# Memory tokens that arrive channels first, packed weight blocks for their projection, x scaled on GpSimd with the norm weight applied at eviction, and half of x transposed between the output products

## The chip, the cores and the metric

The kernel runs on one core of one Trainium2 chip. The metric is the device time of the whole program in microseconds, the median of several executions; lower is better. The engines are named as in the profile: PE (TensorE matmul), PEld (its weight loads), DVE (VectorE), ACT (ScalarE), POOL (GpSimd) and SP (SyncE, which here issues every transfer).

## What is computed

One layer of a hybrid encoder: 1024 tokens of 1024 channels go through a mixer with four head groups (A, B, C, D) and then through cross-attention into 256 memory tokens. The change touches what comes first: the norm of `x`, the keys and values of the memory, and (in the kernel) the product of the values with the output weights.

```python
def rms_norm(x, g):
    y = x32 * lax.rsqrt(jnp.mean(x32 * x32, axis=-1, keepdims=True) + NORM_EPS)
    return (y * g).astype(x.dtype)
...
def memory_cross_attention(h, mem_n, wq, wkv, wo):
    q = split_heads(h @ wq, N_MEM_HEADS)
    k, v = jnp.split(mem_n @ wkv, 2, axis=-1)
    ...
    p = jax.nn.softmax(logits, axis=-1)
    o = jnp.einsum("bhtm,bhmd->bhtd", p.astype(v.dtype), v)
    return merge_heads(o) @ wo
```

The mixer reads `rms_norm(x, pre_norm_g)` through one projection `w_in`. `mem_n` is the memory, 256 x 1024, normed with `mem_norm_g`; `wkv` is 1024 x 2048.

## The kernel before

Every large product is made of three (`mm3`, L136 to L139): both operands are split into a rounded high part and the low rest, and high x high (L137), high x low (L138) and low x high (L139) are added up in PSUM. So each piece of a weight, 256 KB, goes a fixed way (`wload`, L111 to L127): SP loads it to a raw buffer `wr`, ACT casts it to `wh` (L122), and DVE (L124) or POOL (L126) subtracts to make `wl`; in the first stage the two take turns. There are four raw buffers and eight each of `wh` and `wl` there. `split_evac` (L158 to L164) does the same for what comes out of PSUM: ACT makes the high part, DVE the low one, with a factor per partition (L163, L164) or without (L160, L161).

The order of instructions on each engine is set by a list scheduler that follows the written order and priorities, and every engine, SP's transfers included, works strictly in that order. The part up to the mixer runs so:

1. The constants `cols` and two 512 KB row tiles of `mem` are loaded (L188 to L194). PE turns the memory round to channels first, 16 transposes (L215), and `split_evac` writes `mTh` and `mTl` with the norm weight `mg` as factor. ACT squares the row tiles (L220) for the norm of each memory token; two more transposes (L226) bring the 256 factors along the free dimension (`RS`).
2. Eight blocks `cp` (loop at L258) of 256 columns of `wkv`: four weight pieces, 48 products of 256 columns, one multiplication by `RS` (L268), then a store of keys to `kTd` (L270, blocks 0 to 3) or a split of values (blocks 4 to 7). A weight piece is cut out of rows of 2048 columns, 1 KB at a time.
3. In the same loop a tile of 128 tokens of `x` is loaded and normed (`xnorm`, L240): ACT squares and sums, POOL takes the power -0.5 (L143, L144), DVE multiplies by that and by the norm weight in one instruction (`norm_rows`, L151). One block later `xtile` (L247) transposes it, eight transposes into two PSUM banks, and `split_evac` writes `hTh` and `hTl`.
4. Four heads of `vwrow` (L325): 24 products of 512 columns each, values times `wo`, copied out by ACT (L335) and stored.
5. Then comes the first projection of the mixer, group C, which reads all of `hTh` and `hTl`.

PSUM has four banks for products (`mm`) and four for transposes (`tr`) in this stage.

Of the kernel before, what the change touches and what calls it, by code (L numbers as in the profile page):

```python
# [11 lines left out]
ALU = mybir.AluOpType  # L12
# [24 lines left out]
def tile_trunk(ctx: ExitStack, tc: tile.TileContext, a, out, dbg=None):  # L37
# [60 lines left out]
    # ---------------------------------------------------------------- helpers  # L98
# [12 lines left out]
    def wload(src, scale=None):  # L111
        shape = [src.shape[0], src.shape[1], src.shape[2]] if len(src.shape) == 3 else [src.shape[0], src.shape[1]]
        with tc.high_priority():
# [9 lines left out]
            if cur["wp0"] is not None and wcount["wr"] % 2:  # L123
                V.tensor_tensor(lo, raw, f32(hi), op=ALU.subtract)  # L124
            else:
                G.tensor_tensor(lo, raw, f32(hi), op=ALU.subtract)  # L126
# [54 lines left out]
    xp = Pool("xp", {"x": 2, "xn": 3, "gbc": 1})  # L181
    cur["wp0"] = Pool("wp0", {"wr": 2, "wh": 4, "wl": 4})

    # ---------------------------------------------------------------- first loads
    pr0 = tc.cur_priority
    tc.cur_priority = -1000
    cst = base.one("cst", [128, 206])
    SY.dma_start(cst, a["cols"])  # L188
    ident, mg = cst[:, 0:128], cst[:, 198:206]
    mx_ = []  # L190
    for i in range(2):
        x_t = xp("x", [128, 1024])
        SY.dma_start(x_t, a["mem"][0, i * 128:(i + 1) * 128, :])
        mx_.append(x_t)  # L194
# [7 lines left out]
    V.memset(mhalf, -0.5)  # L202

    # ---------------------------------------------------------------- memory side and pre norm
    mss = m0.one("mss", [128, 2])
    mTh = [m0("mT", [128, 4, 256], F32R) for _ in range(2)]
    mTl = [m0("mT", [128, 4, 256], F32R) for _ in range(2)]
    for kp in range(4):
        if kp == 1:
            tc.cur_priority = pr0  # L210
        p = ps("tr", [128, 2, 256])
        for i in range(2):
            for kk in range(2):
                k = 2 * kp + kk
                T.transpose(p[:, kk, i * 128:(i + 1) * 128], mx_[i][:, k * 128:(k + 1) * 128], ident)  # L215
        for kk in range(2):
            q, r = divmod(2 * kp + kk, 4)
            split_evac(mTh[q][:, r, :], mTl[q][:, r, :], p[:, kk, :], mg[:, 2 * kp + kk:2 * kp + kk + 1])
    for i in range(2):
        SC.activation(xp("xn", [128, 1024]), mx_[i], AF.Square, accum_out=mss[:, i:i + 1])  # L220
    mr = rstd_pow("tn", mss, D, EPS, 2)
    rE = m0.one("rE", [128, 2, 128])
    V.tensor_copy(rE, mr[:, :, None].to_broadcast([128, 2, 128]))
    p = ps("tr", [128, 256])
    for i in range(2):
        T.transpose(p[:, i * 128:(i + 1) * 128], rE[:, i, :], ident)  # L226
    RS = m0.one("RS", [128, 2, 256])
    SC.activation(RS[:, 0, :], p, AF.Copy, scale=1.0 / 16)
    SC.copy(RS[:, 1, :], p)
# [1328 lines left out]
```

## Time and profile before

| | |
|---|---|
| time, median of 3 runs | 983.16 us (980.48 to 984.74) |
| span of the profiled execution | 981.5 us (first to last instruction; no separate device time is given for it) |
| mean granted TensorE clock | 0.976 |
| PE busy in 0 to 70 us, by tens | 3.65, 8.70, 9.85, 9.27, 10.00, 10.00, 7.35 us |
| bytes moved by DMA in 0 to 90 us | 21.75 MB, 242 GB/s on average |

The profile is read from the whole to the part: the busy time of each engine over the span, then over stretches of it, then single instructions in order of time. A row of the timeline gives its start, how long it took, the engine, the line, what it wrote from what, and in brackets how long the engine sat idle before it and what ended that. Matmuls overlap, so the distance of their starts tells more than their lengths.

### The profile page before, as it was taken

Reading aid. Unit: us, or ns where it says so; the run is one execution under the profiler, and the core shown is the slowest. Engines: PE = TensorE matmul, PEld = TensorE weight load, DVE = VectorE, ACT = ScalarE, POOL = GpSimd, SP = SyncE. Lnnn points to the kernel's source line nnn. Section 1 sums busy time; section 2 is a strip of 40 time slices with the busy share of each in tenths; the row PEclk is TensorE's granted clock in tenths of the full one; section 3 lists DMA queues with packets and bytes.
Section 4 is the critical chain, followed back from the end, with each engine's and each line's share of the span. In section 5 each row is a group of like instructions: output and inputs, shape, how many; then the busy total and the mean of one; then the engine's idle time right before and its main releaser. Section 6 shows DMA issues by size and latency. Waiting matters only on the chain. (4 is left out here: it accounts for less than half of the span.)

```text
span 981.5 us, 16277 instructions
## 1 busy us (share of the span) xinstructions
PE 929.1 (95%) x6089; PEld 772.7 (79%) x6089; DVE 578.9 (59%) x1291; ACT 419.6 (43%) x974; POOL 252.9 (26%) x254
## 2 busy tenths in 40 slices
PE   6989999797998999999898999999999999999997
PEld 6987887586778877777776776777778788889997
DVE  6773136788696135794498747655556546654226
ACT  6666255231154333653435245433345434443321
POOL 4554224452220224454233412000000000121211
PEclk9999999798999999999899999999999999999999
DMA  7867321102324402322566675432217311125104
GB/s 241 265 212 262 107 54 34 32 22 72 75 66 123 115 28 87 111 80 87 150 158 159 198 258 188 131 100 76 75 46 245 105 35 55 44 67 198 38 12 172
DMA packets 94447, 112.53 MB, mean 115 GB/s; under 512 B 20705, under 2 KB 72993, under 8 KB 94369
## 3 DMA queue, kind: packets, MB, share of 16 engines
q1 hardware_dynamic: 94368, 111.50, 36.5%
q8 instruction: 48, 0.79, 0.3%
q14 instruction: 31, 0.25, 0.1%
HBM read 82.61 MB, written 28.87 MB: 114 GB/s over the span
## 5 line engine op out<-in xcount | busy, mean ns | idle before, releaser
L126 POOL TENSOR_TENSOR wl<-wr,wh 128x512 fp32r<-128x512 f32 (+2 forms) x98 | 139.9, 1430 | 401.8 <-ACT wh L122 385.0
L137 PE MATMUL mm<-h,wh 128*128 128x512 f32 x528 | 219.6, 416 | 0.2 <-DVE zu L754 0.2
L139 PE MATMUL mm<-h,wl 128*128 128x512 f32 x528 | 208.8, 395 | 0.0
L138 PE MATMUL mm<-l,wh 128*128 128x512 f32 x528 | 208.6, 395 | 0.0
L137 PEld LDWEIGHTS mm<-h,wh 128*128 128x128 f32 x528 | 99.9, 189 | 24.3 <-issue 1.9
L139 PEld LDWEIGHTS mm<-h,wl 128*128 128x128 f32 x528 | 99.9, 189 | 22.9
L122 ACT CAST wh<-wr 128x512 fp32r<-128x512 f32 (+2 forms) x122 | 74.7, 619 | 97.5 <-PE mm L138 32.9
L138 PEld LDWEIGHTS mm<-l,wh 128*128 128x128 f32 x528 | 100.2, 190 | 17.4 <-issue 0.5
L137 PE MATMUL mm<-wh,act 128*128 128x256 f32 x256 | 71.7, 280 | 0.0
L138 PE MATMUL mm<-wl,act 128*128 128x256 f32 x256 | 70.9, 277 | 0.0
L139 PE MATMUL mm<-wh,act 128*128 128x256 f32 x256 | 70.8, 277 | 0.0
L137 PE MATMUL mm<-h,act 128*128 128x512 f32 x128 | 54.7, 427 | 0.0
L139 PE MATMUL mm<-h,act 128*128 128x512 f32 x128 | 50.5, 394 | 0.0
L138 PE MATMUL mm<-l,act 128*128 128x512 f32 x128 | 50.4, 394 | 0.0
L137 PEld LDWEIGHTS mm<-wh,act 128*128 128x128 f32 x256 | 48.2, 188 | 0.1
L138 PEld LDWEIGHTS mm<-wl,act 128*128 128x128 f32 x256 | 48.1, 188 | 0.0
L139 PEld LDWEIGHTS mm<-wh,act 128*128 128x128 f32 x256 | 48.0, 188 | 0.0
L137 PE MATMUL mm<-wh,h 128*128 128x260 f32 (+1 forms) x128 | 39.2, 306 | 1.5 <-DVE zu L819 1.5
L137 PE MATMUL mm<-mT,wh 128*128 128x256 f32 x128 | 37.6, 293 | 1.4 <-ACT wh L122 1.4
L139 PE MATMUL mm<-mT,wl 128*128 128x256 f32 x128 | 37.1, 290 | 1.4 <-DVE wl L124 1.4
L139 PE MATMUL mm<-wh,l 128*128 128x260 f32 (+1 forms) x128 | 38.1, 298 | 0.0
L138 PE MATMUL mm<-wl,h 128*128 128x260 f32 (+1 forms) x128 | 38.0, 297 | 0.0
(407 smaller groups left out, 2020.2 us busy)
## 6 DMA issues: line engine op xcount, KB each, us to landing
wr<-in_w_in_dram SPq DMA_DIRECT2D x50, 256.0 KB, 2.9
wr<-in_xattn_wkv_dram SPq DMA_DIRECT2D x32, 256.0 KB, 3.8
x<-in_x_dram SPq DMA_DIRECT2D x16, 512.0 KB, 4.7
x<-x1d SPq DMA_DIRECT2D x15, 512.0 KB, 5.6
wr<-in_xattn_wo_dram SPq DMA_DIRECT2D x16, 256.0 KB, 3.0
vwd<-row SPq DMA_DIRECT2D x8, 512.0 KB, 3.9
rT<-zu SPq DMA_DIRECT2D x16, 256.0 KB, 2.4
zT<-zu SPq DMA_DIRECT2D x16, 256.0 KB, 3.2
```

Of the source, the lines that this page charges most:

```text
L122: SC.copy(hi, raw)
L126: G.tensor_tensor(lo, raw, f32(hi), op=ALU.subtract)
L137: T.matmul(o, lh, rh, start=st, stop=False, skip_group_check=skip)
L138: T.matmul(o, lh, rl, start=False, stop=False, skip_group_check=skip)
L139: T.matmul(o, ll, rh, start=False, stop=sp, skip_group_check=skip)
```

## The change

The host now hands over the memory transposed (`memT`, 128 x 8 x 256) and the memory weights in blocks that lie together (`wkv`, 128 x 8 x 8 x 256, so a piece is 2 KB per partition), and `pre_norm_g` as columns beside `mem_norm_g`. The kernel splits `memT` straight from SBUF. The norm of the memory is made after the first block: ACT squares in place, DVE adds the eight channel groups up, one product with a matrix of ones sums over partitions, and ACT takes logarithm and exponential. `x` is multiplied by its row factor alone, by POOL, into one of six `xn` buffers (two of them held `memT`); the norm weight `pg` becomes the factor of `split_evac`. Transposes of `x` go by channel group, four token tiles to a bank: tokens 0 to 511 behind blocks 4 and 5, tokens 512 to 1023 behind the first two heads of `vwrow`. POOL gets one weight split in three instead of one in two in this stage. Comments and docstrings were taken out.

```diff
                 return hi, lo
             SC.copy(hi, raw)
-            if cur["wp0"] is not None and wcount["wr"] % 2:
+            if cur["wp0"] is not None and wcount["wr"] % 3:
                 V.tensor_tensor(lo, raw, f32(hi), op=ALU.subtract)
             else:
...
     psum(mm=4, tr=4)
     m0 = Pool("m0", {"mT": 4, "KV": 4, "row": 2, "kv": 2})
-    xp = Pool("xp", {"x": 2, "xn": 3, "gbc": 1})
+    xp = Pool("xp", {"x": 2, "xn": 6})
     cur["wp0"] = Pool("wp0", {"wr": 2, "wh": 4, "wl": 4})
     pr0 = tc.cur_priority
     tc.cur_priority = -1000
-    cst = base.one("cst", [128, 206])
+    tc.keep_in_program_order(SC.preload_act_table_set("natural_log_exp_and_others"))
+    cst = base.one("cst", [128, 214])
     SY.dma_start(cst, a["cols"])
-    ident, mg = cst[:, 0:128], cst[:, 198:206]
-    mx_ = []
-    for i in range(2):
-        x_t = xp("x", [128, 1024])
-        SY.dma_start(x_t, a["mem"][0, i * 128:(i + 1) * 128, :])
-        mx_.append(x_t)
+    ident, mg, pg = cst[:, 0:128], cst[:, 198:206], cst[:, 206:214]
+    mraw = [xp("xn", [128, 4, 256]) for _ in range(2)]
+    wv = a["wkv"]
+    wk0 = []
+    for q in range(4):
+        SY.dma_start(mraw[q // 2][:, q % 2 * 2:q % 2 * 2 + 2, :], a["memT"][:, 2 * q:2 * q + 2, :])
+        wk0.append(wload(wv[:, 0, 2 * q:2 * q + 2, :]))
     jp = m0.one("jp", [128, 128], mybir.dt.int32)
     G.iota(jp, pattern=[[1, 128]], base=0, channel_multiplier=-1)
...
     mhalf = base.one("mhalf", [128, 4])
     V.memset(mhalf, -0.5)
-    mss = m0.one("mss", [128, 2])
+    onesa = m0.one("onesa", [128, 128])
+    V.memset(onesa, 1.0)
     mTh = [m0("mT", [128, 4, 256], F32R) for _ in range(2)]
     mTl = [m0("mT", [128, 4, 256], F32R) for _ in range(2)]
-    for kp in range(4):
-        if kp == 1:
-            tc.cur_priority = pr0
-        p = ps("tr", [128, 2, 256])
-        for i in range(2):
-            for kk in range(2):
-                k = 2 * kp + kk
-                T.transpose(p[:, kk, i * 128:(i + 1) * 128], mx_[i][:, k * 128:(k + 1) * 128], ident)
-        for kk in range(2):
-            q, r = divmod(2 * kp + kk, 4)
-            split_evac(mTh[q][:, r, :], mTl[q][:, r, :], p[:, kk, :], mg[:, 2 * kp + kk:2 * kp + kk + 1])
-    for i in range(2):
-        SC.activation(xp("xn", [128, 1024]), mx_[i], AF.Square, accum_out=mss[:, i:i + 1])
-    mr = rstd_pow("tn", mss, D, EPS, 2)
-    rE = m0.one("rE", [128, 2, 128])
-    V.tensor_copy(rE, mr[:, :, None].to_broadcast([128, 2, 128]))
-    p = ps("tr", [128, 256])
-    for i in range(2):
-        T.transpose(p[:, i * 128:(i + 1) * 128], rE[:, i, :], ident)
+    for k in range(8):
+        q, r = divmod(k, 4)
+        split_evac(mTh[q][:, r, :], mTl[q][:, r, :], mraw[q][:, r, :], mg[:, k:k + 1])
+    tc.cur_priority = pr0
     RS = m0.one("RS", [128, 2, 256])
-    SC.activation(RS[:, 0, :], p, AF.Copy, scale=1.0 / 16)
-    SC.copy(RS[:, 1, :], p)
-    pg = gload(xp, "gbc", a["pre_norm_g"][0])
+    def memnorm():
+        for q in range(2):
+            SC.activation(mraw[q], mraw[q], AF.Square)
+        V.tensor_tensor(mraw[0], mraw[0], mraw[1], op=ALU.add)
+        V.tensor_tensor(mraw[0][:, 0:2], mraw[0][:, 0:2], mraw[0][:, 2:4], op=ALU.add)
+        V.tensor_tensor(mraw[0][:, 0], mraw[0][:, 0], mraw[0][:, 1], op=ALU.add)
+        p = ps("tr", [128, 256])
+        T.matmul(p, onesa, mraw[0][:, 0], start=True, stop=True)
+        SC.activation(RS[:, 1, :], p, AF.Ln, bias=eps_n, scale=1.0 / D)
+        SC.activation(RS[:, 1, :], RS[:, 1, :], AF.Exp, scale=-0.5)
+        SC.activation(RS[:, 0, :], RS[:, 1, :], AF.Copy, scale=1.0 / 16)
     hTh = [hT("h", [128, 4, 512], F32R) for _ in range(4)]
     hTl = [hT("l", [128, 4, 512], F32R) for _ in range(4)]
...
         SY.dma_start(x_t, a["x"][0, i * 128:(i + 1) * 128, :])
         xn = xp("xn", [128, 1024])
-        norm_rows(x_t, pg, xn)
-        return xn
-    def xtile(i, xn):
-        ts = slice(i % 4 * 128, (i % 4 + 1) * 128)
-        for q in range(2):
+        r = base("tn", [128, 1])
+        SC.activation(xn, x_t, AF.Square, accum_out=r)
+        r = rstd_pow("tn", r, D, EPS)
+        G.tensor_scalar(xn, x_t, r, None, op0=ALU.mult)
+        xn_.append(xn)
+    def xhalf(hf, k0, nk):
+        for k in range(k0, k0 + nk):
             p = ps("tr", [128, 4, 128])
-            for k in range(4):
-                T.transpose(p[:, k, :], xn[:, (4 * q + k) * 128:(4 * q + k + 1) * 128], ident)
-            w = 2 * (i // 4) + q
-            split_evac(hTh[w][:, :, ts], hTl[w][:, :, ts], p)
+            for i in range(4):
+                T.transpose(p[:, i, :], xn_[4 * hf + i][:, k * 128:(k + 1) * 128], ident)
+            w = 2 * hf + k // 4
+            split_evac(hTh[w][:, k % 4, :], hTl[w][:, k % 4, :], p.rearrange("p a b -> p (a b)"), pg[:, k:k + 1])
     Vh = [m0("KV", [128, 4, 256], F32R) for _ in range(2)]
     Vl = [m0("KV", [128, 4, 256], F32R) for _ in range(2)]
-    xn_ = {}
-    xn_[0] = xnorm(0)
+    xn_ = []
     for cp in range(8):
         p = ps("mm", [128, 2, 256])
-        for k, wh, wl in wpiece(a["xattn_wkv"][0], cp * 256, 256, 2):
+        for k in range(8):
+            if k % 2 == 0:
+                wp = wk0[k // 2] if cp == 0 else wload(wv[:, cp, k:k + 2, :])
+            wh, wl = (w_[:, k % 2, :] for w_ in wp)
             for c in range(2):
                 cs = slice(c * 128, (c + 1) * 128)
                 mm3(p[:, c, :], wh[:, cs], wl[:, cs], mTh[k // 4][:, k % 4, :], mTl[k // 4][:, k % 4, :],
                     k == 0 and c == 0, k == 7, True)
+        if cp == 0:
+            memnorm()
         t = m0("kv", [128, 2, 256])
         V.tensor_tensor(t, p, RS[:, cp // 4, None, :].to_broadcast([128, 2, 256]), op=ALU.mult)
...
             q, r = divmod(2 * cp - 8, 4)
             split_evac(Vh[q][:, r:r + 2, :], Vl[q][:, r:r + 2, :], t)
-        if cp < 7:
-            xn_[cp + 1] = xnorm(cp + 1)
-        if cp > 0:
-            xtile(cp - 1, xn_[cp - 1])
-    xtile(7, xn_[7])
+        xnorm(cp)
+        if cp in (4, 5):
+            xhalf(0, 4 * cp - 16, 4)
     incl = m0.one("incl", [128, 128])
     V.tensor_scalar(incl, jp, 0.0, None, op0=ALU.is_ge)
...
         nxt = vwprep(h + 1) if h < 3 else None
         vwrow(h, w)
+        if h < 2:
+            xhalf(1, 4 * h, 4)
         w = nxt
     w_in = a["w_in"][0]
...
     wp3.close()
     base.close()
-_INS = ["x", "mem", "pre_norm_g", "post_norm_g", "w_in", "b_in", "norm_a_g", "decay_w2", "iclr_a2", "gn_c_g", "gn_c_b",
-        "w_out", "xattn_post_g", "xattn_wq", "xattn_wkv", "xattn_wo", "cols", "poolbd"]
+_INS = ["x", "memT", "post_norm_g", "w_in", "b_in", "norm_a_g", "decay_w2", "iclr_a2", "gn_c_g", "gn_c_b",
+        "w_out", "xattn_post_g", "xattn_wq", "wkv", "xattn_wo", "cols", "poolbd"]
 def _pack(a):
     import numpy as np
...
             a["decay_w0"][0], a["iclr_a0"][0], a["key_k"][0], a["key_a"][0], a["bonus_u"][0],
             np.tile(a["qk_norm_d"][0], (1, 2)), b[O_AZ:O_AZ + 256], b[O_BZ:O_BZ + 256], b[O_CZ:O_CZ + 256], b[O_DZ:O_DZ + 256],
-            a["xattn_pre_g"][0], a["pool_scale"][0], b[O_DQ:O_DQ + 512], a["mem_norm_g"]]
+            a["xattn_pre_g"][0], a["pool_scale"][0], b[O_DQ:O_DQ + 512], a["mem_norm_g"], a["pre_norm_g"][0]]
     cols = np.concatenate([np.asarray(r).reshape(-1, 128) for r in rows], axis=0).T
     w = np.asarray(a["pool_w"][0])
...
         r0 = (g % 2) * 64
         pw[r0:r0 + 64, g // 2, r0:r0 + 64] = w[g]
-    return {"cols": np.concatenate([np.eye(128, dtype=cols.dtype), cols], axis=1), "poolbd": pw}
+    mt = np.asarray(a["mem"][0]).T.reshape(8, 128, 256).transpose(1, 0, 2)
+    wkv = np.asarray(a["xattn_wkv"][0]).reshape(8, 128, 8, 256).transpose(1, 2, 0, 3)
+    return {"cols": np.concatenate([np.eye(128, dtype=cols.dtype), cols], axis=1), "poolbd": pw, "memT": mt, "wkv": wkv}
 def kernel(**inputs):
```

Three places show how the order of instructions moves. In the rows, `tr`, `mm` and `KV` are banks of transposes, banks of products and the split values; the number behind a name tells buffers apart.

On ACT at the start of the program, before:

```order
L220 ACT_TABLE_LOAD
L220 ACTIVATE xn_149,mss<-x_98 128x1024
L163 ACTIVATE mT_109<-tr_113,cst 128x256
L163 ACTIVATE mT_109<-tr_122,cst 128x256
L220 ACTIVATE xn_151,mss<-x_100 128x1024
L163 ACTIVATE mT_109<-tr_113,cst 128x256
L122 CAST wh_190<-wr_188 128x512
L122 CAST wh_208<-wr_206 128x512
```

and of the change (`xn_99` and `xn_100` hold the transposed memory):

```order
L187 ACT_TABLE_LOAD
L163 ACTIVATE mT_137<-xn_99,cst 128x256 x4
L163 ACTIVATE mT_138<-xn_100,cst 128x256 x4
L122 CAST wh_104<-wr_102 128x512
L220 ACTIVATE xn_99<-xn_99 128x1024
L220 ACTIVATE xn_100<-xn_100 128x1024
L122 CAST wh_111<-wr_109 128x512
L122 CAST wh_118<-wr_116 128x512
```

All eight evictions of the memory now stand ahead of the first weight cast, where three stood, and the two Squares stand between the first cast and the second.

On PE behind the last block of the memory projection, before (`xn_748` and `xn_848` are the normed token tiles 6 and 7):

```order
L139 MATMUL mm_869<-mT_110,wl_927 128x256
L252 MATMUL tr_946<-cst,xn_748 128x128 x4
L252 MATMUL tr_953<-cst,xn_748 128x128 x4
L252 MATMUL tr_960<-cst,xn_848 128x128 x4
L252 MATMUL tr_967<-cst,xn_848 128x128 x4
L137 MATMUL mm_1057<-wh_1010,KV_174 128x512
```

and of the change, behind the first head's output products, the first of four such banks (`xn_575` to `xn_889` are token tiles 4 to 7):

```order
L139 MATMUL mm_1005<-wh_950,KV_168 128x512
L253 MATMUL tr_1014<-cst,xn_575 128x128
L253 MATMUL tr_1014<-cst,xn_689 128x128
L253 MATMUL tr_1014<-cst,xn_803 128x128
L253 MATMUL tr_1014<-cst,xn_889 128x128
L253 MATMUL tr_1021<-cst,xn_575 128x128
```

The transposes have moved from the place between the memory projection and the output products to places between heads of the output products, and each bank now takes a piece of four token tiles.

On POOL near the start, before:

```order
L126 TENSOR_TENSOR wl_209<-wr_206,wh_208 128x512
L126 TENSOR_TENSOR wl_245<-wr_242,wh_244 128x512
L143 TENSOR_SCALAR tn_183<-tn_181 128x1
L144 TENSOR_TENSOR tn_183<-tn_183,mhalf 128x1
L126 TENSOR_TENSOR wl_294<-wr_291,wh_293 128x512
```

and of the change (`x_232` and `x_317` are the raw token tiles 0 and 1):

```order
L126 TENSOR_TENSOR wl_119<-wr_116,wh_118 128x512
L143 TENSOR_SCALAR tn_237<-tn_235 128x1
L144 TENSOR_TENSOR tn_237<-tn_237,mhalf 128x1
L245 TENSOR_SCALAR xn_234<-x_232,tn_237 128x1024
L143 TENSOR_SCALAR tn_322<-tn_320 128x1
L144 TENSOR_TENSOR tn_322<-tn_322,mhalf 128x1
L245 TENSOR_SCALAR xn_319<-x_317,tn_322 128x1024
L126 TENSOR_TENSOR wl_263<-wr_260,wh_262 128x512
```

The multiply of each token tile stands behind its norm on POOL, and two of them stand ahead of the second weight split there.

## The prediction

> **What bounds the kernel now.** I read the summary of engines first, then the busy time by stretches for the first 90 us, where all edited lines run, and then the timeline of the places where TensorE (PE) is not full.
>
> ```profile
> PE 929.1 (95%) x6089; PEld 772.7 (79%) x6089; DVE 578.9 (59%) x1291; ACT 419.6 (43%) x974; POOL 252.9 (26%) x254
> ...
> 0.00:10.00 10.00, 3.65 (x16) 3.27 (x16) 3.46 (x24) 4.96 (x9) 1.00 (x8) 1.00 0.81 269
> 10.00:20.00 10.00, 8.70 (x51) 8.14 (x52) 8.04 (x12) 7.55 (x17) 5.66 (x7) 1.00 0.67 233
> ...
> 60.00:70.00 10.00, 7.35 (x63) 7.11 (x61) 8.70 (x11) 5.92 (x11) 5.97 (x5) 1.00 0.46 147
> 70.00:80.00 10.00, 8.65 (x29) 6.92 (x30) 7.99 (x12) 7.95 (x15) 3.15 (x2) 0.66 0.51 175
> ```
>
> The kernel is bound by PE, 95% busy. So I count PE time alone, up to one mark: the first product of the C projection. Behind the mark the order of instructions is row for row the same, and I take the shift of the mark as the shift of the end. In the stretches (columns behind the length: PE, weight loads, DVE, ACT, POOL, clock, DMA share, GB/s) PE is weak at two places: the first 12 us, and 60 to 80 us, where the granted clock also falls to 0.66.
>
> ```profile
> 5.28 3.65 PE L215 MATMUL tr<-cst,x 128*128 128x128 f32 x16 [5.28 <-DMA x<-in_mem_dram]
> 10.33 0.58 PE L137 MATMUL mm<-mT,wh 128*128 128x256 f32 x1 [1.40 <-ACT wh L122]
> 12.75 0.58 PE L139 MATMUL mm<-mT,wl 128*128 128x256 f32 x1 [0.52 <-DVE wl L124]
> 13.13 0.41 PE L137 MATMUL mm<-mT,wh 128*128 128x256 f32 x1
> ...
> 15.69 0.42 PE L137 MATMUL mm<-mT,wh 128*128 128x256 f32 x1
> 16.54 0.28 PE L138 MATMUL mm<-mT,wh 128*128 128x256 f32 x1
> ...
> 18.08 0.28 PE L139 MATMUL mm<-mT,wl 128*128 128x256 f32 x1
> ...
> 20.21 0.28 PE L139 MATMUL mm<-mT,wl 128*128 128x256 f32 x1
> ...
> 30.73 0.39 PE L139 MATMUL mm<-mT,wl 128*128 128x256 f32 x1 [0.88 <-DVE wl L124]
> ...
> 40.09 1.03 PE L252 MATMUL tr<-cst,xn 128*128 128x128 f32 x8
> 46.55 1.04 PE L252 MATMUL tr<-cst,xn 128*128 128x128 f32 x8
> ...
> 64.72 1.28 DVE L151 SCALAR_TENSOR_TENSOR xn<-x,tn,gbc 128x1024 f32<-128x1024 f32 x1 [0.95 <-POOL tn L144]
> 65.92 3.45 DVE L124 TENSOR_TENSOR wl<-wr,wh 128x512 fp32r<-128x512 f32 x2
> 69.30 0.68 DVE L268 TENSOR_TENSOR kv<-mm,RS 128x512 f32<-128x512 f32 x1
> 69.90 0.67 DVE L161 TENSOR_TENSOR l<-tr,h 128x512 fp32r<-128x512 f32 x1
> 70.63 0.66 PE L252 MATMUL tr<-cst,xn 128*128 128x128 f32 x4 [3.28 <-DVE l L161]
> 72.01 1.11 PE L252 MATMUL tr<-cst,xn 128*128 128x128 f32 x4 [0.72 <-DVE l L161]
> 72.77 0.78 PE L137 MATMUL mm<-wh,KV 128*128 128x512 f32 x1
> ...
> 74.20 0.63 PE L137 MATMUL mm<-wh,KV 128*128 128x512 f32 x1
> 75.48 0.63 PE L137 MATMUL mm<-wh,KV 128*128 128x512 f32 x1
> 78.01 0.40 PE L137 MATMUL mm<-wh,KV 128*128 128x512 f32 x1
> ...
> 80.11 0.40 PE L137 MATMUL mm<-wh,KV 128*128 128x512 f32 x1
> 87.12 0.40 PE L137 MATMUL mm<-wh,KV 128*128 128x512 f32 x1
> 97.62 0.39 PE L137 MATMUL mm<-h,wh 128*128 128x512 f32 x1
> ```
>
> What the reader is to see, from top to bottom:
> - The mark stands at 97.62. The first weight product of the memory projection runs at 10.33, and PE runs without a break only from 12.75, two products in.
> - Until about 16.4 a 256-wide product takes (15.69 - 13.13) / 12 = 0.213 us from start to start, afterwards (20.21 - 18.08) / 18 = 0.118: the array runs at half speed for 3.6 us of steady work. (The clock column shows 1.00 there, the starts don't.)
> - One block of 48 products and 8 transposes takes 46.55 - 40.09 = 6.46 us; 48 x 0.118 = 5.68, so a transpose is 0.10.
> - At 67.35 PE stops for 3.28 and then 0.72 us. The transposes of the last token tiles want a PSUM bank whose eviction (`l`, L161) is queued on VectorE (DVE) behind a norm multiply that waited for GpSimd, and two weight splits of 1.7 us each. After the stop the clock is halved: 512-wide products at (75.48 - 74.20) / 3 = 0.427 us until 78.0, then (87.12 - 80.11) / 30 = 0.234.
>
> PE's need at full speed is therefore 8 x 6.46 + 96 x 0.234 = 51.7 + 22.4 = 74.1 us. From 12.75 to the mark pass 84.9. Of the 10.8 in excess, the slow start holds 17 x 0.095 = 1.6, the wait at 30.73 0.9, the stop 4.0, and the slow clock behind it 12 x 0.193 = 2.3 plus about 1.0 in the transposes; 1.0 I can't place.
>
> **The change, part by part.**
>
> ```profile
> 5.17 1.06 ACT L220 ACTIVATE xn<-x 128x1024 f32<-128x1024 f32 x1 [3.17 <-DMA x<-in_mem_dram]
> ...
> L122 ACT CAST wh<-wr 128x512 fp32r<-128x512 f32 x52 | 31.4, 620 | 15.1 <-DMA wr<-in_xattn_wkv_dram 10.0 <-DMA wr<-in_w_in_dram 2.2 <-DMA wr<-in_xattn_wo_dram 1.4
> ...
> L163 ACT ACTIVATE mT<-tr,cst 128x256 fp32r<-128x256 f32 x8 | 3.4, 472 | 2.9 <-DVE mT L164 1.7 <-PE tr L215 1.2
> ...
> L124 DVE TENSOR_TENSOR wl<-wr,wh 128x512 fp32r<-128x512 f32 x24 | 27.6, 1154 | 9.1 <-ACT wh L122 9.1
> L151 DVE SCALAR_TENSOR_TENSOR xn<-x,tn,gbc 128x1024 f32<-128x1024 f32 x8 | 12.3, 1538 | 7.5 <-POOL tn L144 7.4
> ...
> L126 POOL TENSOR_TENSOR wl<-wr,wh 128x512 fp32r<-128x512 f32 x90 | 127.7, 1422 | 378.5 <-ACT wh L122 362.0 <-ACT gates L741 7.4 <-DVE wl L124 6.6
> ...
> L144 POOL TENSOR_TENSOR tn<-tn,mhalf 128x1 f32<-128x1 f32 x8 | 4.3, 541 | 0.7
> ...
> L592 POOL MEMSET n<- 128x1024 f32 x1 | 1.0, 952 | 0.0
> ```
>
> *Start.* The 16 memory transposes go (3.65 us at half speed, all before the first product). The same megabyte of `mem` lands in quarters; the row at 5.17 shows its first tile there, and I estimate the last quarter between 5.2 and 6.7 us. ACT then does eight evictions straight from SBUF, 8 x 0.47 = 3.8, from about 3.5 to 7.3 (to 7.6 if the last quarter is late), and the first cast, 0.62: the first product can start near 8.0 instead of 10.33. But ACT's next two instructions are the Squares of the memory, 1.06 each, ahead of the second cast; that cast ends near 10.7. DVE's sum of squares (1024 wide, twice the unhindered 0.68 of a 512-wide one, 1.4) holds the second low part to about 12.0. PE does the 12 products of the first piece and one or two of the second, waits about 1 us, and is continuous from 12.0 with 13 products done, against 12.75 with 2. With the same 3.6 us of slow clock that is 0.75 + 11 x 0.118 = 2.0 us ahead. Bounds: 0.5 (late quarter, a cast behind it) to 4 (clock released during the first piece).
>
> *Norm of the memory.* One ones product replaces two transposes; only the first sum waits for it, with three free PSUM banks ahead of PE. Its price on PE lies between a 256-wide start-to-start, 0.12, and the whole length of one, 0.58 at 10.33; I take 0.4, near the upper end, since its operands aren't split.
>
> *Transposes of x.* 64 before, 64 after: no PE time saved. Half stand behind blocks 4 and 5, half between the output products.
>
> *The stop at 67.35.* The norm multiply leaves DVE: 8 x 1.54 = 12.3 us. DVE takes 32 of the 48 weight splits instead of 24: 8 x 0.68 to 1.15, 5.4 to 9.2 back. What counts is the order: the last 32 transposes now follow 24 output products (5.6 us) each, and the 16 evictions of the earlier ones have blocks of 5.7 us to finish in, at about 0.6 (ACT) and 0.7 (DVE) each, four at a time. I take the whole stop, 4.0, and the slow clock behind it, 3.3, as gone. What is late next is the last scaled x tile. Tiles 6 and 7 take the buffers of tiles 0 and 1, free behind the second run of 16 transposes, by the count below at 61.0 - 2 x 5.7 = 49.6 us; two Squares, norms and multiplies of about 3.3 together follow, so they are ready near 57, and needed 5.6 us behind block 7, at 66.6.
>
> *GpSimd (POOL).* It gains eight 1024-wide multiplies by a column. No row shows one. The nearest are a 1024-wide fill at 0.95, which only writes, and the two-input split, 1.42 for 512, so 2.84 for 1024. I take 1.3, nearer the fill, since only one tensor is read. It gives up a third of its splits: 16 of 48 instead of 24. A block of 5.7 us then holds 1.33 x 1.42 + 0.8 (the norm's power at 0.54 and a smaller step ahead of it) + 1.3 = 4.0 us, at 2.84 still 5.5. Behind each multiply wait the next split on POOL and, through the raw buffer, SP's next load; behind SP's waiting load wait the x tile and the K row. I count nothing on PE, because the cover is the loader's lead: the weight pieces are two blocks deep. If that lead is gone, each late split is a PE wait of up to 2.8.
>
> [...]
>
> *Packed weights.*
>
> ```profile
> wr<-in_xattn_wkv_dram SPq DMA_DIRECT2D x32, 256.0 KB, 3.8
> wr<-in_xattn_wo_dram SPq DMA_DIRECT2D x16, 256.0 KB, 3.0
> ...
> SPq L115 <- POOL wl L126: 24.7, 15, 3.6
> ```
>
> A piece comes in 2 KB rows, as `w_out` pieces do: 3.0 us to landing instead of 3.8. SP's wait for those splits shows that the loop of four raw buffers (load, cast, split, load) is nearly as long as a block, so 0.8 less helps it keep up with blocks that shrink from 6.46 to 5.7 us. On PE: 0 to 0.9 (the wait at 30.73). I take 0.
>
> *Sum.* Start 2.0, minus 0.4, stop 4.0, clock 3.3: 8.9; a full count with no wait left (12.0 + 74.1 - 13 x 0.118 + 1.6 + 0.4 = 86.6 against 97.62; block 7 ends there at 86.6 - 22.4 - 3.2 = 61.0) gives 11.0. I forecast 9.4: of the 1.9 between them (the wait at 30.73 and the part that I can't place) most stays. The profiled span is 981.5, which lies 1.7 below the median of the runs, 983.16; no other time is given for that execution, so I take the shift off the median: **973.8 us**, about 1% less.
>
> **Rivals.**
> - *The loader falls behind* in blocks 1 to 3, which have no transposes to cover it. If the loop stays at 6.3 us, PE waits 0.6 in each, and the first split behind two x multiplies costs 2.8 more: gain 5 to 6, near 977.5. ACT's casts waiting 10 us for DMA speak for it, the two-block lead and shorter landings against.
> - *The stop comes back elsewhere.* If one of the four runs of 16 transposes (1.6 us each) must wait for a bank or the last x tile for some 3 us, the stop and the slow clock return: gain 9.4 - 7.3 = 2.1, near 981. The row at 70.63 speaks for it, the spacing above against. [...]
> - *POOL becomes the bound* (slower). Six multiplies, six norm pairs and nine splits stand ahead of the last memory split: 12.8 + 6 x 0.8 + 9 x 1.42 + 6 X = 30.3 + 6 X, needed near 59. With X the time of a multiply, the 11 us of gain are eaten at X = 6.7, and at 7.5 the kernel is near 988. That is 2.6 times the dearest row, so unlikely.
> - *More than forecast*: the clock is released early and no wait is left, gain 11 to 13, near 971.
>
> **How the numbers follow.** Forecast 0.62, loader 0.15, stop elsewhere 0.13, POOL bound 0.04, more 0.06. Half a per cent, about what a measurement of this kernel can tell from no change, is 4.9 us. Faster by more: 0.62 + 0.15 + 0.06 = 0.83; within: 0.13; slower: 0.04. The range takes in the start's bounds, the loader case and most of the upper one: 969.5 to 980.0.
>
> **What would show it.** The mark near 87 to 89 us; PE's first product near 8 with one wait of about 1 us; no PE wait of over 1 us between 13 and 85 and full-speed starts throughout the output products; POOL's new multiply between 0.95 and 2.84; DVE under 7 of 10 busy from 20 to 60 us. Wrong would be: a wait of PE at a transpose of x, a mark behind 92, or a mark at 88 with the end not moved by as much.

## The result and the profile after

The changed kernel is slower: 992.52 us, median of 4 runs (990.84 to 993.76), beside 982.19 for the kernel before on the same chip (4 runs, 980.48 to 984.74). The ratio is 1.0101, 95% interval 1.0075 to 1.0128. The profiled execution took 992.3 with a span of 990.5; the one of before has a span of 981.5, so the two profiles differ by 9.0, and the medians by 10.3.

First the page's summary of engines, then the stretches (columns as in the prediction) and PE's waits from the start to 130 us (total, times, longest).

```profile
PE 933.8 (94%) x6073; PEld 775.7 (78%) x6073; DVE 567.2 (57%) x1294; ACT 420.7 (42%) x973; POOL 257.8 (26%) x252
```

```profile
0.00:10.00 10.00, 1.19 (x4) 0.97 (x5) 6.30 (x30) 6.49 (x12) 0.58 (x6) 1.00 0.78 255
10.00:20.00 10.00, 8.73 (x47) 8.44 (x47) 7.98 (x12) 6.67 (x12) 7.56 (x7) 1.00 0.72 228
20.00:30.00 10.00, 8.96 (x74) 8.70 (x73) 2.68 (x4) 5.13 (x10) 8.51 (x7) 1.00 0.64 214
30.00:40.00 10.00, 8.55 (x73) 8.34 (x71) 3.88 (x5) 5.20 (x10) 6.64 (x8) 1.00 0.72 242
40.00:50.00 10.00, 8.30 (x72) 8.10 (x71) 3.95 (x6) 5.04 (x9) 9.26 (x6) 1.00 0.80 267
...
70.00:80.00 10.00, 4.26 (x14) 3.07 (x13) 2.50 (x4) 2.16 (x5) 8.16 (x6) 0.82 0.27 77
```

```profile
PE mm L137 <- ACT wh L122: 8.8, 1, 8.8
PE mm L138 <- POOL wl L126: 5.7, 1, 5.7
PE mm L139 <- POOL wl L126: 4.2, 3, 1.7
PE mm L139 <- DVE wl L124: 1.3, 1, 1.3
...
```

In every stretch shown between 20 and 80 us POOL is the busiest engine beside PE (in two of them busier than PE), and DVE has time to spare (2.5 to 4.0 of 10). There PE waits for one thing, the low parts of weights that POOL makes: 9.9 us in four waits. The groups of instructions on POOL in the first 110 us say why, and the timeline shows the waits themselves:

```profile
L126 POOL TENSOR_TENSOR wl<-wr,wh 128x512 fp32r<-128x512 f32 x21 | 27.4, 1314 | 45.4 <-ACT wh L122 42.6 <-DVE wl L124 2.7
L245 POOL TENSOR_SCALAR xn<-x,tn 128x1024 f32<-128x1024 f32 x8 | 23.0, 2870 | 0.8
```

```profile
8.81 0.58 PE L137 MATMUL mm<-mT,wh 128*128 128x256 f32 x1 [8.81 <-ACT wh L122]
13.73 0.58 PE L139 MATMUL mm<-mT,wl 128*128 128x256 f32 x1 [1.27 <-DVE wl L124]
...
19.06 2.86 POOL L245 TENSOR_SCALAR xn<-x,tn 128x1024 f32<-128x1024 f32 x1
21.88 2.51 POOL L126 TENSOR_TENSOR wl<-wr,wh 128x512 fp32r<-128x512 f32 x2
23.20 0.39 PE L139 MATMUL mm<-mT,wl 128*128 128x256 f32 x1 [1.04 <-POOL wl L126]
...
66.65 1.06 ACT L243 ACTIVATE xn<-x 128x1024 f32<-128x1024 f32 x1
68.83 2.92 POOL L245 TENSOR_SCALAR xn<-x,tn 128x1024 f32<-128x1024 f32 x1
69.03 0.40 PE L137 MATMUL mm<-wh,KV 128*128 128x512 f32 x1
71.12 0.40 PE L137 MATMUL mm<-wh,KV 128*128 128x512 f32 x1
73.12 2.85 POOL L245 TENSOR_SCALAR xn<-x,tn 128x1024 f32<-128x1024 f32 x1
75.94 2.49 POOL L126 TENSOR_TENSOR wl<-wr,wh 128x512 fp32r<-128x512 f32 x2
77.25 0.79 PE L138 MATMUL mm<-wl,KV 128*128 128x512 f32 x1 [5.74 <-POOL wl L126]
79.89 0.62 ACT L122 CAST wh<-wr 128x512 fp32r<-128x512 f32 x1 [7.45 <-DMA wr<-in_xattn_wo_dram]
103.58 0.39 PE L137 MATMUL mm<-h,wh 128*128 128x512 f32 x1
```

SP, which loads the pieces, waited for POOL's splits like this up to 130 us (total, times, longest):

```profile
SPq L115 <- POOL wl L126: 52.6, 18, 7.8
```

What is to be seen: the multiply takes 2.87 us, and the split behind it starts when it ends (19.06 + 2.86 = 21.9); PE resumes when the first of two splits is done. The large stop is the same thing with the multiplies of the last two token tiles (68.83 and 73.12) ahead of one split. Their Squares came late on ACT (66.65), so they stood in the queue just when the output products began. The raw buffers that the two splits held kept SP from loading for 7.8 us (in sum SP waits no more for POOL's splits than before, 53.2 us in 27 waits; it waits less often and longer), ACT's cast then waited 7.45 us for its piece, and PE ran 13 products at half speed after the stop (from 77.25 to 83, 0.43 us from start to start, 0.23 from 85 on). The mark, the first product of the C projection, stands at 103.58 instead of 97.62: **+5.96**, where the forecast had -9.4.

The shift of the mark isn't the whole. Behind the mark it wanders between about 4.7 and 6.5, is 6.0 again where the last 768 products begin (885.88 against 879.84), and there grows to 9.1. In the output stage at the end, 256-wide products stand in a row; first the kernel before, then the changed one, one product of the same line and a later one:

```profile
940.11 0.28 PE L137 MATMUL mm<-wh,act 128*128 128x256 f32 x1
...
945.21 0.28 PE L137 MATMUL mm<-wh,act 128*128 128x256 f32 x1
```

```profile
949.10 0.28 PE L137 MATMUL mm<-wh,act 128*128 128x256 f32 x1
...
954.06 0.28 PE L137 MATMUL mm<-wh,act 128*128 128x256 f32 x1
```

Before, 45 products lie between the two rows, (945.21 - 940.11) / 45 = 0.1133 us each; after, 42 lie there, (954.06 - 949.10) / 42 = 0.1181. For 768 products these 4 to 5 ns are 3 to 4 us; from the first to the last of them pass 95.2 us before and 98.2 after. No instruction of this stage was changed, but the constants tile `cst` had grown from 206 to 214 columns, so every tile placed behind it lies 32 bytes further on. 6.0 + 3.0 is the difference of the two profiles.

### The profile page after: what moved, and what is told of

It reads as the page before. It is cut to its first block, busy times and chain, and to the rows that moved or that the text cites. A ratio compares the mean times of both kernels' runs of the same rounds, so it can differ in the third digit from the quotient of the medians.

```text
span 990.5 us, 16243 instructions
## 1 busy us (share of the span) xinstructions
PE 933.8 (94%) x6073; PEld 775.7 (78%) x6073; DVE 567.2 (57%) x1294; ACT 420.7 (42%) x973; POOL 257.8 (26%) x252
## 5 line engine op out<-in xcount | busy, mean ns | idle before, releaser
L126 POOL TENSOR_TENSOR wl<-wr,wh 128x512 fp32r<-128x512 f32 (+2 forms) x90 | 122.0, 1358 | 417.5 <-ACT wh L122 400.0
L137 PE MATMUL mm<-wh,act 128*128 128x256 f32 x256 | 72.7, 284 | 0.0
L139 PE MATMUL mm<-wh,act 128*128 128x256 f32 x256 | 71.8, 281 | 0.0
L124 DVE TENSOR_TENSOR wl<-wr,wh 128x512 fp32r<-128x512 f32 x32 | 25.4, 798 | 36.8 <-ACT wh L122 36.7
```

The lines of the kernel that those rows point to most:

```text
L137: T.matmul(o, lh, rh, start=st, stop=False, skip_group_check=skip)
L139: T.matmul(o, ll, rh, start=False, stop=sp, skip_group_check=skip)
```

## The experiments

Twelve more runs were made. "Mark" is the start of the first product of the C projection, as a shift against 97.62; "pace" is the median start-to-start of the 256-wide products at the end; the ratio is to the kernel before, measured alongside (medians of 981.5 to 982.6 us), with its 95% interval.

```
kernel                 mark    pace ns   time us   ratio to before
before                  0        113     982.2     1
changed kernel        +5.96      117     992.52    1.0101 (1.0075 to 1.0128)
x_on_dve              -4.55      117     982.64    0.9983 (0.9962 to 1.0003)
xn_8_buffers          +3.3       117     988.11    1.0051 (1.0032 to 1.0070)
memory_part_alone     +0.3       117     983.21    0.9993 (0.9972 to 1.0013)
before_cst_214       -0.9         117     984.14    1.0013 (0.9992 to 1.0033)
before_again          -0.44      113     982.47    (one execution)
splits_on_dve         -7.5       117     976.05    0.9942 (0.9923 to 0.9961)
x_on_dve_206          -4.55      113     979.62    0.9978 (0.9960 to 0.9996)
spread_transposes     -7.1       113     978.01    0.9960 (0.9939 to 0.9980)
half_splits_on_pool  +12.0       117     994.48    1.0117 (1.0085 to 1.0148)
splits_on_dve_206     -7.8       113     974.56    0.9921 (0.9898 to 0.9944)
splits_206_spread    -10.0       113     974.23    0.9914 (0.9890 to 0.9938)
after_cst_238         +6.8       118     990.45    1.0095 (1.0078 to 1.0112)
```

Single executions of one kernel spread by 3 to 4 us either way, so a profile's span can lie that far from the median; marks and waits are read from one profile each. Up to 3 us of a mark come from the start, where the array begins at half speed (256-wide products start every 0.21 us, then every 0.12): in the changed kernel, `xn_8_buffers` and `memory_part_alone` the full pace came at 18.3 to 19.0 us, in the eight other variants of the change at 12.3 to 15.4, and PE's 64th instruction began at 21.9 to 22.4 against 19.3 to 20.2. The edits don't explain all of this: `after_cst_238` runs the changed kernel's instructions, and its 64th began 1.95 us earlier.

### x scaled by VectorE

```diff
-        G.tensor_scalar(xn, x_t, r, None, op0=ALU.mult)
+        V.tensor_scalar(xn, x_t, r, None, op0=ALU.mult)
```

> The changed kernel with one edit: the multiply of x by its row factor is done by DVE instead of POOL. Theory 1 (the multiply, 2.87 us on POOL, holds back the weight splits queued behind it, they hold SP's loads, and PE starves): the waits of PE for POOL splits (4.2 us in blocks 1 to 4), the stop of 5.7 us at 71.5 and the slow clock behind it (about 3.7) go; the mark (first C product, 103.6 in the changed kernel, 97.6 before) comes to 88 to 91 and the time to 977 to 980. Theory 2 (not the length of the multiply but the place of the last two tiles, whose buffers come free only behind the second run of transposes): a stop of 3 us or more stays at the output products, mark 95 or later, 984 or more.

The mark moved by 10.5 us against the changed kernel, to 93.07, and no wait for POOL was left. Of the 10.5, 2.1 lie in the start: the full pace came at 12.4, before the first multiply begins at 14.7. Mark and time missed theory 1's ranges by 2 to 3 us, on the slow side. The waits, one stretch, and the transposes in it show what came next in line:

```profile
PE tr L253 <- DVE l L164: 2.5, 2, 1.8
PE mm L139 <- DVE wl L124: 2.2, 2, 1.3
...
50.00:60.00 10.00, 7.53 (x52) 6.85 (x51) 8.71 (x13) 8.31 (x15) 1.98 (x3) 0.83 0.83 263
...
52.06 1.31 PE L253 MATMUL tr<-cst,xn 128*128 128x128 f32 x8 [1.77 <-DVE l L164]
54.06 1.08 PE L253 MATMUL tr<-cst,xn 128*128 128x128 f32 x4 [0.69 <-DVE l L164]
```

The run of 16 transposes behind block 5 needs four banks, and the evictions of the run behind block 4 stand on ACT and DVE among casts and splits that wait for their transfers. From 49.65 to 54.80 PE had no product, and the granted clock of the stretch is 0.83. This is the prediction's second rival, at work as soon as POOL no longer held PE up.

### Eight buffers for scaled x

```diff
-    xp = Pool("xp", {"x": 2, "xn": 6})
+    xp = Pool("xp", {"x": 2, "xn": 8})
```

> The changed kernel with eight xn buffers instead of six, so no x tile waits for the transposes of another; the multiply stays on POOL. Theory 1: POOL has the same work, so the waits for splits stay or move: 987 to 993. Theory 2: the stop at 71.5 and its slow clock (9.4 us together) go: 981 to 985.

With no tile waiting for a buffer, the last two multiplies no longer fall on the start of the output products. The big stop went, the short waits stayed, and one of them halved PE's pace for 3.4 us (a product every 0.21 us from 39.4 on instead of every 0.12):

```profile
PE mm L139 <- POOL wl L126: 6.3, 4, 2.4
...
39.03 0.58 PE L139 MATMUL mm<-mT,wl 128*128 128x256 f32 x1 [1.97 <-POOL wl L126]
```

The result, 988.11, lies in the range of theory 1, near its lower end: the late tiles explain 4 to 5 us of the time. The rest, the waits on POOL's queue and the slower end, stays without them.

### The memory's part alone

Here `memT`, the packed weights, the new memory norm and the split ratio of the change stand with the old treatment of `x` (DVE multiplies by both factors, eight transposes a block).

```diff
-        G.tensor_scalar(xn, x_t, r, None, op0=ALU.mult)
-        xn_.append(xn)
...
+        norm_rows(x_t, pg, xn)
+        return xn
...
-        if cp in (4, 5):
-            xhalf(0, 4 * cp - 16, 4)
...
+        if cp > 0:
+            xtile(cp - 1, xn_[cp - 1])
```

> The change's memory part alone: transposed memory, packed weights, norm by logarithm, one split in three on POOL; x as before (norm and weight by one DVE instruction, eight transposes per block, no factor at eviction). Theory 1 (the x part does the harm): not slower than before; the start gives about 2 us, the stop at 67 may stay: 976 to 982. Rival (the memory part costs too: Squares ahead of the second cast, more splits on DVE): 984 or more.

```profile
PE tr L251 <- DVE l L161: 2.6, 2, 1.9
PE mm L139 <- POOL wl L126: 1.7, 1, 1.7
PE mm L139 <- DVE wl L124: 1.7, 2, 1.3
```

The time is that of the kernel before, 1.2 us above the range expected for theory 1. The 13th product starts 2.9 us earlier than before, but by the 36th the lead is gone, because the half pace lasts until 19.0 here and until 16.5 there; later waits for splits follow, and the stop at the last transposes is back. So the memory's part neither did the harm nor, alone, any good that can be measured.

### The wider constants tile, and before once more

The kernel before with `cst` at 214 columns, and the kernel before unchanged.

> The kernel before with the tile of constants 214 columns wide instead of 206, which moves the addresses of the tiles behind it and changes nothing else. In the profiles the 256-wide output products at the end start every 117 ns in the changed kernel and every 113 before, 3 us over 768 of them. Rival A (the addresses): 117 ns here too and 985. Rival B (it differs from execution to execution or comes from elsewhere): 113 ns and 982.

> The kernel before, unchanged, for a second profile. The 256-wide output products at the end started every 113 ns in the first profile and every 117 ns in all five others, whose constants tile is 214 wide. Rival A (the addresses of the tiles decide): 113 ns again. Rival B (it differs from execution to execution): 117 ns, and the first profile of before was a lucky one.

With the wide tile the same program runs the products at the end at 117 ns, in the second profile of the kernel before they start every 113 to 114. The median lies 1.5 us above that of the kernel before beside it, but the interval of the ratio reaches below 1, so the price isn't shown by this pair of times. The unchanged kernel also stopped for 4.3 us at the last transposes again, so that stop is no accident of one execution.

### All weight splits of the first stage on VectorE

```diff
-            if cur["wp0"] is not None and wcount["wr"] % 3:
+            if cur["wp0"] is not None:
```

The multiply stays on POOL, as long as before: this tells its place on x's own path from what stands behind it in the queue.

> The changed kernel with all weight splits of the first stage on DVE; POOL keeps the multiply of x (2.87 us each) and the small norm steps. Theory 1a (the harm is that splits queue behind the multiply on POOL and hold the raw buffers and SP): PE's waits for POOL splits go and the mark comes to 90 to 96, the time to 979 to 986, though POOL's multiply is as long as before. Theory 1b (the x tiles themselves come too late because the multiply is long): PE waits at transposes instead, mark 98 or later, 987 or more.

PE's waits behind the first product, two stretches, and the group of the multiplies on POOL:

```profile
PE tr L253 <- DVE l L164: 2.7, 1, 2.7
PE mm L139 <- DVE wl L124: 0.2, 1, 0.2
...
20.00:30.00 10.00, 10.00 (x85) 9.81 (x84) 5.11 (x8) 5.79 (x11) 7.11 (x6) 1.00 0.93 321
30.00:40.00 10.00, 10.00 (x87) 10.00 (x86) 6.82 (x10) 4.97 (x10) 7.73 (x5) 1.00 0.96 331
...
L245 POOL TENSOR_SCALAR xn<-x,tn 128x1024 f32<-128x1024 f32 x8 | 25.5, 3192 | 0.8
```

The multiply now takes even longer, 3.19 us, and PE is full all the same. DVE makes 16 more splits and is still not at its limit (5.1 to 6.8 of 10 here); the DMA engines go from 0.64 to 0.93 busy, as is to be expected where no split that waits behind a multiply holds a raw buffer (SP's longest wait for a split between 10 and 75 us is 2.4 us, on DVE; in the changed kernel 5.1, on POOL). The kernel is faster than before, 976.05, and faster than the 979 to 986 expected.

### More splits on GpSimd

The opposite dose: 24 of the 48 splits on POOL, as before the change.

```diff
-            if cur["wp0"] is not None and wcount["wr"] % 3:
+            if cur["wp0"] is not None and wcount["wr"] % 2:
```

> The changed kernel with 24 instead of 16 of the first stage's 48 weight splits on GpSimd; the multiply of x stays there. If the harm is GpSimd's queue (splits behind 2.87 us multiplies hold raw buffers, SP and PE), eight more splits of 1.3 us there make it worse than the changed kernel: the mark of the C projection behind 104 us, waits of PE on GpSimd's low parts of 13 us or more together in the first 110 us (10 in the changed kernel), time 993 us or more, ratio to the kernel before 1.010 to 1.017. If the harm came from VectorE or ACT instead (their queues hold the transposes' evictions), VectorE has 8 x 1.15 us less to do and the mark comes earlier than 103.6, time under 992.

```profile
PE mm L139 <- POOL wl L126: 10.3, 5, 5.2
PE mm L138 <- POOL wl L126: 6.8, 1, 6.8
...
20.00:30.00 10.00, 5.11 (x24) 5.11 (x25) 1.99 (x3) 2.87 (x6) 9.62 (x8) 0.67 0.51 148
```

Waits for POOL rose from 9.9 to 17.1 us, and the mark fell back to 109.66. With 16, 24 and no splits behind the multiplies the mark moves by +6.0, +12.0 and -7.5. Counted from PE's 64th instruction, and so without the start, the way to the mark takes 81.7, 90.3 and 70.8 us. DVE is idle for 8 us of the stretch shown, so a shortage of DVE is ruled out.

### The narrow tile again, and smaller runs of transposes

`pg` gets a tile of its own that is given back after the first stage, so `cst` keeps 206 columns:

```diff
-    cst = base.one("cst", [128, 214])
-    SY.dma_start(cst, a["cols"])
-    ident, mg, pg = cst[:, 0:128], cst[:, 198:206], cst[:, 206:214]
+    cst = base.one("cst", [128, 206])
+    SY.dma_start(cst, a["cols"][:, 0:206])
+    ident, mg = cst[:, 0:128], cst[:, 198:206]
+    pg = xp.one("pgc", [128, 8])
...
+    SY.dma_start(pg, a["cols"][:, 206:214])
```

with x on VectorE, and with the splits on VectorE:

> x_on_dve with the norm weight in a tile of its own that is given up after the first stage, so the constants tile is 206 wide as before. Addresses decide: 113 ns at the end and about 3 us less than x_on_dve, 979 to 980. They don't: 117 ns and 982 to 983.

> The changed kernel with all weight splits of the first stage on VectorE, and with the constants tile 206 columns wide as before (the norm weight columns in a tile of their own that is given back after the stage). Theory: two causes that add up. GpSimd's queue is off PE's path (mark near 90), and the 256-wide products at the end start every 113 to 114 ns instead of 117 (3 us over 768 of them). Expected: mark 89.5 to 91, 972 to 974 us, ratio 0.990 to 0.993, which is 3 us under the same kernel with the wide tile (976.05). Rival: the 3 us between the two tile widths are chance or belong to x on VectorE alone; then 975 to 977 us and a start-to-start of 117 ns.

The pace at the end is 113 ns in both, and the medians are 3.0 and 1.5 us under those with the wide tile; the second lies 0.6 above the range expected. The kernel before moved too, by 0.9 and 0.1, and by the ratios the gains are 0.5 and 2.1 us, neither clear of the intervals: the price of the wide tile stands in the profiles, not in these times.

On top of each came eight `xn` buffers and transposes in runs of 8 and 12 instead of 16:

```diff
-        if cp in (4, 5):
-            xhalf(0, 4 * cp - 16, 4)
+        if cp > 3:
+            xhalf(0, 2 * cp - 8, 2)
...
-        if h < 2:
-            xhalf(1, 4 * h, 4)
+        if h < 3:
+            xhalf(1, 3 * h, 3 if h < 2 else 2)
```

> x_on_dve_206 with eight xn buffers and the transposes spread: two banks behind each of blocks 4 to 7, three, three and two banks behind the first three heads. In x_on_dve PE waits 2.5 us for evictions inside the second run of 16 transposes and the clock then halves, some 5 us in all; theory 1 with rival 2 of the prediction says these go: mark 88 to 89 (93 in x_on_dve), 4 to 5 us less than x_on_dve_206. If the lost time has another cause: within 2 us of x_on_dve_206.

> As the one before, and eight xn buffers, with the transposes of x in smaller runs: two banks behind each of the blocks 4 to 7, three, three and two behind the first three heads. Theory: the 2.7 us that PE still waited for a bank at the transposes of the first half go, because eight transposes need two banks and four are there: mark 87 to 89, 970 to 972 us. Rival, as with x on VectorE, where the same spreading gained 1.6 us: what is won by the first output product is lost behind it to waits for weights, mark 89 to 90, 972 to 973 us.

With x on VectorE the mark came to 90.51, not to the 88 to 89 expected, and the time gained 1.6 us instead of 4 to 5. With the splits on VectorE the mark came to 87.66, where it was expected; the waits in the first 115 us and two of the stretches are

```profile
PE mm L137 <- ACT wh L122: 9.7, 1, 9.7
PE mm L137 <- DVE rk L487: 1.2, 1, 1.2
...
40.00:50.00 10.00, 10.00 (x88) 10.00 (x88) 7.45 (x12) 8.05 (x15) 5.38 (x6) 1.00 0.92 301
50.00:60.00 10.00, 10.00 (x88) 10.00 (x87) 9.20 (x13) 6.84 (x13) 6.63 (x4) 1.00 0.69 202
```

PE has no wait from its first product, at 9.67, to the mark. Still the time is 974.23, above the 970 to 972 expected and no better, as far as these runs can tell, than the 974.56 without the spreading: 2.2 us gained at the mark, of which 1.2 go to a new wait 15 us behind it (L487). Both kernels beat the kernel before by 0.8 to 0.9%.

### Does the byte position decide?

`cst` at 238 columns, of which 214 are used: tiles behind it move by 128 bytes in all, and the `wh` tiles of the last stage lie as far from a 128-byte line as before the change.

```diff
-    cst = base.one("cst", [128, 214])
-    SY.dma_start(cst, a["cols"])
+    cst = base.one("cst", [128, 238])
+    SY.dma_start(cst[:, 0:214], a["cols"])
```

> The changed kernel with the constants tile made 238 columns wide, of which 214 are used: every tile placed behind it moves by 96 bytes more, which is 128 bytes in all against the kernel before. Nothing else differs. If the slower end of the changed kernel (256-wide products every 117 ns instead of 113 to 114) hangs on where the tiles lie within 128 bytes, the products start every 113 to 114 ns again, the shift against the kernel before no longer grows by 3 us over the end, and the time is 988.5 to 990.5 us (ratio 1.006 to 1.009) with the mark still near 103.5. Rival: it hangs on something else that goes with the wider tile or the changed program; then 117 ns and 991 to 994 us as in the changed kernel. If the theory of GpSimd's queue is right, the mark stays near 103.5 in both cases.

That theory fell: the pace is 117 to 118 ns, though the time, 990.45, lies in its range; the mark is +6.8. So it isn't the position within 128 bytes. The profiles show something more: 113 and 117 are two paces that PE falls into. In the kernel before, the first 120 to 180 of these products (two profiles) start every 117 to 118 ns and the rest every 113 to 114; with 238 columns, some stretches near the beginning run at 113 and the rest at 117 to 118. Six of six profiles with 206 columns settle at the fast pace, eight of eight with more settle at the slow one. What decides it stays open.

## Why the prediction was wrong

- **The step that failed** is POOL's: "I take 1.3, nearer the fill, since only one tensor is read", and "I count nothing on PE, because the cover is the loader's lead: the weight pieces are two blocks deep." The multiply measured 2.87, just above the dear bound of 2.84. The size alone didn't do it: with the splits on DVE it took 3.19 and the mark came 7.5 us early. What cost the time was its place in the queue. The text had named what stands behind it (the next split, and through the raw buffer SP's next load), priced it at up to 2.8 us each, and then set it to nothing. There were four such waits, 1.0, 1.5, 1.7 and 5.7, each ended by a split that had started when a multiply ended (21.88, 36.42, 42.66 and 75.94).
- **The cover was no cover.** Two blocks of lead hold only while the loader runs free. A split that waits holds its raw buffer; so the lead shrinks with each multiply, and with it SP's, ACT's and PE's (the DMA engines were 0.64 busy from 20 to 30 us, and 0.93 with all splits on DVE). The rival that had POOL as bound added up busy time and broke even at 6.7 us (6.6 by its own terms); by that sum 2.87 was harmless, and POOL was in fact busy only 53% of the first 100 us. A queue in order did its harm by delay here, long before it was full.
- **The choice near the fill**, "since only one tensor is read", didn't hold: 2.87 for a 128x1024 multiply by a column is 2.80 ns for each element of a row, where the two-input split takes 1.31 for 512, 2.57. On DVE the same multiply took 0.74 to 0.76 in five of eight cases, and about 1.77 in the three others (x on DVE).
- **The start** was forecast 2.0 us ahead; at 18.4 us it was level with before, 36 products done in both. The first product came at 8.81 (forecast 8.0) and the wait behind the first piece was there as described, but it ended at 13.73, not 12.0: DVE's split of the second piece ran beside one on POOL and took 1.77. The products ran at half speed for 3.4 us ahead of that wait and for 4.6 behind it, until 18.3, where 3.6 were forecast in all. When the pace doubles is in part luck: the same instructions had it at 12.3 in `after_cst_238`, and the kernel before at 16.5 in one profile and 18.3 in the other.
- **The stop at 67.35** did go from the transposes of x, as forecast, and came back as a stop of output products: 5.74 us and the slow clock behind it, 2.8. Tiles 6 and 7 were forecast ready near 57 and were ready at 71.7 and 76.0. They weren't late for their transposes; their multiplies were in the way of a split.
- From the full count (86.6) the mark lies 17.0 us late: start 2.2 (the 62nd product began at 21.9, by the forecast's steps at 19.7), three short waits 4.2, the stop 5.9 with its restart, slow clock 2.8 (13 products by 0.19, and the first by 0.36); some 1.9 I can't place.
- **The end** was taken as shifted by the mark. That failed by 3.0 us in the pair of profiles, the slower pace behind the wider tile, which no step considered.
- **Transposes and the clock.** The slow start was read off one profile, in which the 16 transposes with which PE's work begins take 3.65 us, one starting every 0.21 to the last. In the second profile of the kernel before they take 3.31 us, because the last of them start every 0.11 us, and the granted clock rises at 8.02, ahead of the first product and with nothing but transposes on PE until then; from 10 to 20 us it is 0.66 on average.

```profile
5.19 3.31 PE L215 MATMUL tr<-cst,x 128*128 128x128 f32 x16 [5.19 <-DMA x<-in_mem_dram]
```

- What held: transposes of x saved no PE time but ran free of waits (0.2); DVE had room; and the second rival's mechanism was real, it appeared once x was scaled on DVE. The packed pieces landed in 3.6 us (3.8 before), not in 3.0. The experiment that takes out the failed step and the wide tile, splits on DVE with 206 columns, gave 974.56. Against the kernel before beside it, 981.61, that is a gain of 7.1 us, or 7.8 by the ratio, where 9.4 were forecast: it comes near, and the closeness of 974.56 to the 973.8 forecast is in part the luck of a lower baseline.

## What to carry to other kernels

When work moves to an engine that executes in order, price it by what stands behind it and whose buffers that holds, not by the engine's busy share: here an engine 53% busy cost PE 10 us of waits. Where a duration is known only between two bounds, work out at the dear end not only the busy time but also what stands behind it, and see which cover fails first. And compare the pace of unchanged stages before and after: with a tile that grew by 32 bytes, the pace of one went from 113 to 117 ns here.

## What the runs showed of the hardware

- **Two paces.** 256-wide products that nothing holds up start every 113 or every 117 to 118 ns, at the same granted clock of 1.00, in stretches of one profile (the kernel before: 118 up to about 900 us, 113 from 908 to 975).
- **DVE and POOL.** In the changed kernel, on DVE and then on POOL:

```profile
30.15 1.21 DVE L124 TENSOR_TENSOR wl<-wr,wh 128x512 fp32r<-128x512 f32 x1 [1.47 <-ACT wh L122]
34.86 0.69 DVE L124 TENSOR_TENSOR wl<-wr,wh 128x512 fp32r<-128x512 f32 x1 [1.13 <-ACT wh L122]
...
29.51 1.30 POOL L126 TENSOR_TENSOR wl<-wr,wh 128x512 fp32r<-128x512 f32 x1 [1.22 <-ACT wh L122]
33.53 2.91 POOL L245 TENSOR_SCALAR xn<-x,tn 128x1024 f32<-128x1024 f32 x1
```

  A DVE split that starts inside a POOL split takes 1.21 instead of 0.69 and ends 0.55 behind it (30.15 + 1.21 against 29.51 + 1.30): it is held until about the POOL split's end. The seven other DVE splits of the first 110 us that start inside a POOL split end 0.54 to 0.60 behind it too. One that starts inside POOL's multiply takes 0.69 and isn't held up; nor was any other of the twelve that met only a multiply in this kernel. With all splits on DVE a multiply that began at 24.23, inside a DVE split with a second right behind it (23.75 to 25.04), took 3.46 us, while the changed kernel's at 25.42, with two splits inside it that start later, took 2.86. Three splits in the kernel with all of them on DVE took 1.35 to 1.56 beside a multiply, which I can't explain.
- **The clock.** The length of a wait alone doesn't tell whether the clock falls. In the kernel before, the wait of 3.28 us up to 70.63 was followed by a granted clock of 0.50 from 71.14 to 77.97; in the changed kernel it was 0.50 from 76.34 to 83.16, around the end of the wait of 5.74 at 77.25. A wait of 1.97 us halved the pace for 3.4 us (eight buffers: granted clock 0.95 from 30 to 40 us, 0.88 from 40 to 50), and one of 2.75 did not (half the splits on POOL: 1.00 from 40 to 50). In two cases transposes stand beside the wait: after 5.15 us without a product, with waits of 1.77 and 0.69 in them, products started every 0.21 us until 56.8 (x on DVE, granted clock 0.83 from 50 to 60); after 4.58 us, with one wait of 2.72, they started every 0.12 (splits on DVE, 1.00). What decides between them isn't shown.
